# Two plain blocks in place of three at the start of channel mixers 2 to 4, with the Newton steps on GpSimd

## The chip, the core and the metric

The kernel runs on one core of one Trainium2 chip. The metric is the device time of one execution in microseconds (us); lower is better. The core has a matrix engine (TensorE, PE in the profile, with its weight loads as PEld), three vector-like engines (VectorE = DVE, ScalarE = ACT, GpSimd = POOL), an engine that issues transfers (SyncE = SP), and 16 DMA engines between the device memory and the on-chip memory (SBUF). Matmuls write to PSUM, which has 8 banks.

## The reference

A decoder trunk of two layers over 512 positions and 1024 features. Each layer has a channel mixer, a token mixer (latent attention in layer 0, sparse attention in layer 1) and a second channel mixer:

```python
h = h + 0.5 * swiglu(rmsnorm(h, g_a), ...)
h = h + mixer(rmsnorm(h, g_m), ...)
h = h + 0.5 * swiglu(rmsnorm(h, g_b), ...)
def rmsnorm(x, g): return x * rsqrt(mean(x * x, -1) + 1e-6) * g
def swiglu(x, w_gate, w_up, w_down):      # 1024 -> 2816 -> 1024
    return (silu(x @ w_gate) * (x @ w_up)) @ w_down
```

So there are four channel mixers, called mixer 1 to 4 here (`idx` 0 to 3 in the code). The whole is in float32.

## The kernel before

*Layout.* The residual `h` lies as 8 chunks of 128 features by 512 positions. A channel mixer (`ffn`) has 22 blocks `f` of 128 hidden features; each block has a gate and an up product, each of a 1024 x 128 weight slab with all positions.

*Precision.* Every operand is split into a high part (ScalarE's copy to a shorter float format) and a low part (VectorE subtracts the high part), in `split` and `slab_ahead`. A product is then three matmuls: high-high, high-low, low-high.

*Two kinds of blocks.* In a *plain* block (`plain`, `plain1`, L401 to L403) gate and up are computed directly: 2 slabs x 8 chunks x 2 halves of 256 positions x 3 matmuls. In the other blocks (`wsums`, `product`, L386 to L388) gate and up together are seven products of quarter size, in the manner of Strassen and Winograd, each of 4 chunk pairs x 3 matmuls of 256 positions. For these `combine(p)` forms sums of the activations of chunk pair p (`y`, `u`, `four`; L267 to L273 and a split), once per mixer, and `wsums` forms sums of each block's weights (L372 to L376) and splits them. Products 1, 6 and 5 go through one bank (`px`) and 7 and 4 through another (`pq`), with copies by ScalarE between (L554 to L561); 2 and 3 end in the gate's bank (`pg`).

*Norm.* The activations go into the products with the gain but without the norm's factor. Its sums of squares are collected chunk by chunk (`sumsq`, ScalarE and GpSimd); the last two chunks of a mixer's input come in `late`, which ends in small matmuls `pc` and `rsqrt_col`. `rsqrt` makes a first guess from the bits and takes three Newton steps on a 128 x 4 tile (L299 to L304, all on VectorE). `norm_bcast` spreads the column with four transposes (`pb`, L323) and ScalarE copies it to `row`. `gate` multiplies the gate's result by `row`, takes Silu, and multiplies again; `act` forms the hidden activations and splits them.

*Start of a mixer.* The first `PLAIN` = 3 blocks are plain, their gates' banks all held until the row is there; behind them stand the gates, and the combines lie in blocks 0, 1 and 2. In mixer 1 the positions' sums of squares come from a second copy of the input. From block 3 on, each third block (`f % NG == 0`) opens eight `unit`s of the down product of the last three blocks, which are shared out over three blocks; the last blocks' down products stand at the mixer's end, where the next mixer's input is prepared chunk by chunk.

*What sets the order.* Each engine works through a fixed queue. The queues are made by a planner when the program is built: it goes through the program's instructions with the written order as priority, and an engine takes the first that its model holds ready. `issue_after` adds a rule on top: the splits of the block after the first block of products are issued behind `evicted`, the last copy out of `px` in the block before (L561, L365). Transfers of weights are issued by SyncE.

Of the kernel before, what the change touches and what calls it, by code (L numbers as in the profile page):

```python
# [48 lines left out]
PLAIN = 3  # L49
# [12 lines left out]
class Kern:  # L62
# [228 lines left out]
    def rsqrt(self, y, v, t, psum, n):  # L291

        nc = self.nc
        nc.vector.tensor_scalar(v, psum, 1.0 / n, EPS, op0=ALU.mult, op1=ALU.add)
        self.newton(y, v, t)

    def newton(self, y, v, t):
        nc = self.nc
        nc.vector.tensor_scalar(y.bitcast(I32), v.bitcast(I32), 1, None, op0=ALU.logical_shift_right)  # L299
        nc.vector.tensor_scalar(y.bitcast(I32), y.bitcast(I32), -1.0, float(0x5F3759DF), op0=ALU.mult, op1=ALU.add)  # L300
        for _ in range(3):
            nc.vector.scalar_tensor_tensor(t, y, -0.5, v, op0=ALU.mult, op1=ALU.mult)
            nc.vector.tensor_tensor(t, t, y, op=ALU.mult)
            nc.vector.scalar_tensor_tensor(y, t, 1.5, y, op0=ALU.add, op1=ALU.mult)  # L304

# [35 lines left out]
    def wsums(self, idx, f):  # L341
# [3 lines left out]
        if f == PLAIN:  # L345
# [10 lines left out]
        def split(src, pool, tag, bufs):  # L356
# [8 lines left out]
            with self.tc.issue_after(self.evicted.ins) if f == PLAIN + 1 else nullcontext():  # L365
# [61 lines left out]
    def ffn(self, idx, gain_next, ap, tp):  # L427
        nc, a = self.nc, self.a
        self.scr, self.fp = (tp, "sq", 1), tp
# [14 lines left out]
        def act(f):  # L444
            t = tu[f]
            if f < PLAIN:
# [51 lines left out]
        gates = [self.bank("T", "pg") for _ in range(PLAIN)]  # L498
        for f, g in enumerate(gates):
# [12 lines left out]
            if f == 0 and idx > 1:  # L512
                col = late()
            if f == 1 and idx == 0:
                squares(2)
                squares(3)
                col = self.rsqrt_col(sums, D)
            if idx or f:
                self.plain(idx, f, 1, u)
            if f == 0 and idx == 1:  # L520

                col = late()
            if f == 1:
                nc.scalar.activation(self.tiny[:, 4:5], col[:, 0:1], AF.Silu, scale=-1.0)
                pb = self.norm_bcast(col)
                row = tp.tile([P, S], F32, tag="row", bufs=1, name="row")
                self.spread = nc.scalar.activation(row, pb, AF.Copy)
# [6 lines left out]
            for p in (((0,), (1,), (2, 3)) if idx else ((0, 1), (2,), (3,)))[f]:  # L534
                self.combine(p)
# [3 lines left out]

        tail = PLAIN + (NF - 2 - PLAIN) // NG * NG  # L540
        for f in range(PLAIN, NF):
            if f % NG == 0 and f <= tail:
# [991 lines left out]
```

## Time and profile before

| | |
|---|---|
| median of three runs | 1863.17 us (1862.06 to 1864.02) |
| profiled execution | 1862.05 us, its span 1860.3 us |
| granted TensorE clock | 0.999 of full |
| TensorE busy | 1845.7 us (99%), 14464 matmuls |
| VectorE busy | 1507.4 us (81%) |
| ScalarE busy | 1064.5 us (57%) |
| GpSimd busy | 296.7 us (16%) |

Mixer 1 runs from the start to some 355 us, mixer 2 from 546 to 881, mixer 3 from 881 to some 1213, mixer 4 from 1513 on. A row of the instructions in order of time gives the start, the duration, the engine, the source line, the operation, the tile written <- the tiles read, and their shapes; in square brackets stands the idle time of the engine before it and what ended it. Matmuls are pipelined, so their durations overlap; what one costs is read from start to start. Line numbers are those of the kernel before.

### The profile page before, as it was taken

How to read it: one execution, taken by the hardware profiler on the slowest of the kernel's cores; microseconds unless marked ns; L12 is line 12 of the kernel's file. 1: busy time of each engine (PE TensorE's matmuls, PEld its weight loads, DVE VectorE, ACT ScalarE, POOL GpSimd, SP SyncE). 2: the span in 40 equal slices, each digit the busy share in tenths (PEclk: the TensorE clock that was granted, in tenths of full speed). 3: DMA queues.
4: the chain of work that ended last, by engine and by line, in shares of the span. 5: the costliest groups of instructions: out<-in, count | busy, mean ns of one | idle time of the engine just before them, and what ended most of it. 6: DMA issues, size and time to landing. Idle time of an engine off the chain costs nothing.

```text
span 1860.3 us, 37031 instructions
## 1 busy us (share of the span) xinstructions
PE 1845.7 (99%) x14464; PEld 1763.4 (95%) x14464; DVE 1507.4 (81%) x2810; ACT 1064.5 (57%) x1997; POOL 296.7 (16%) x370
## 2 busy tenths in 40 slices
PE   9999999999999999999999999999999999999998
PEld 9999999888889999999999999988888889999997
DVE  8988886688779988886898888666878888888885
ACT  7555553567666555554655545446776865555554
POOL 0000000258830000001000000022666620000000
PEclk9999999999999999999999999999999999999999
DMA  6433331434433433322443332162433133433321
GB/s 238 132 108 103 103 92 48 117 105 103 114 123 112 119 103 109 110 73 72 138 118 110 109 106 81 45 183 82 108 108 103 40 118 116 121 104 107 103 78 69
DMA packets 84351, 196.64 MB, mean 106 GB/s; under 512 B 10944, under 2 KB 38464, under 8 KB 84176
## 3 DMA queue, kind: packets, MB, share of 16 engines
q1 hardware_dynamic: 81664, 191.34, 34.9%
q10 hardware_dynamic: 2512, 2.93, 0.5%
q8 instruction: 114, 1.87, 0.4%
q14 instruction: 61, 0.50, 0.1%
HBM read 178.44 MB, written 2.16 MB: 97 GB/s over the span
## 4 chain that ended last, share of the span: by engine, by line
PE 93%; DVE 3%; ACT 1%; issue 1%; POOL 1%; DMA 0%; ACTq 0%; POOLq 0%; DVEq 0%
PE pd L462 8%; PE pd L464 8%; PE pd L463 8%; PE px L386 6%; PE px L388 6%; PE px L387 5%; PE pg L386 4%; PE pg L388 4%; PE pg L387 4%; PE pq L386 4%; PE pq L388 4%; PE pq L387 4%; PE o L1337 2%; PE pt L1310 2%; PE po L197 2%; PE po L199 2%
## 5 line engine op out<-in xcount | busy, mean ns | idle before, releaser
L462 PE MATMUL pd<-ah,wd 128*128 128x256 f32 x1152 | 318.3, 276 | 0.0
L464 PE MATMUL pd<-ah,wd 128*128 128x256 f32 x1152 | 318.3, 276 | 0.0
L463 PE MATMUL pd<-al,wd 128*128 128x256 f32 x1152 | 318.3, 276 | 0.0
L289 POOL TENSOR_TENSOR s<-s,sq 128x512 f32<-128x512 f32 x38 | 54.7, 1441 | 1050.3 <-ACT sq L285 1050.3
L462 PEld LDWEIGHTS pd<-ah,wd 128*128 128x128 f32 x1152 | 216.3, 188 | 0.0
L464 PEld LDWEIGHTS pd<-ah,wd 128*128 128x128 f32 x1152 | 216.3, 188 | 0.0
L463 PEld LDWEIGHTS pd<-al,wd 128*128 128x128 f32 x1152 | 216.3, 188 | 0.0
L206 DVE TENSOR_TENSOR w<-wr,w 128x1024 fp32r<-128x1024 f32 x72 | 88.2, 1225 | 120.7 <-ACT w L205 120.4
L386 PE MATMUL px<-four,wh 128*128 128x256 f32 x608 | 168.4, 277 | 0.4 <-ACT wh L205 0.2
L388 PE MATMUL px<-four,wl 128*128 128x256 f32 x608 | 168.2, 277 | 0.2 <-DVE wl L206 0.2
L386 PE MATMUL pq<-four,wh 128*128 128x256 f32 x608 | 168.1, 276 | 0.2 <-ACT uq L556 0.2
L387 PE MATMUL px<-four,wh 128*128 128x256 f32 x608 | 168.0, 276 | 0.0
L388 PE MATMUL pq<-four,wl 128*128 128x256 f32 x608 | 167.9, 276 | 0.0
L387 PE MATMUL pq<-four,wh 128*128 128x256 f32 x608 | 167.9, 276 | 0.0
L468 DVE SCALAR_TENSOR_TENSOR h<-pd,h 128x512 f32<-128x512 f32 x216 | 148.3, 686 | 15.4 <-PE pd L464 15.2
L205 ACT ACTIVATE wd<-wdr 128x384 fp32r<-128x384 f32 x192 | 99.2, 519 | 103.8 <-issue 64.6
L176 ACT ACTIVATE w<-wr 128x1024 fp32r<-128x1024 f32 (+3 forms) x89 | 80.8, 908 | 87.5 <-PE pd L464 20.6
L206 DVE TENSOR_TENSOR wd<-wdr,wd 128x384 fp32r<-128x384 f32 x192 | 105.8, 553 | 20.1 <-ACT wd L205 20.0
L178 DVE TENSOR_TENSOR w<-wr,w 128x1024 fp32r<-128x1024 f32 (+3 forms) x75 | 78.3, 1044 | 50.0 <-ACT w L176 49.8
L728 ACT ACTIVATE p<-p,small 128x512 f32<-128x512 f32 (+2 forms) x192 | 106.9, 558 | 19.0 <-DVE small L727 15.3
L386 PEld LDWEIGHTS px<-four,wh 128*128 128x128 f32 x608 | 114.1, 188 | 1.0 <-ACT wh L205 0.4
L388 PEld LDWEIGHTS px<-four,wl 128*128 128x128 f32 x608 | 114.2, 188 | 0.6 <-DVE wl L206 0.6
(379 smaller groups left out, 6264.9 us busy)
## 6 DMA issues: line engine op xcount, KB each, us to landing
wr<-in_w_gu SPq DMA_DIRECT2D x93, 512.0 KB, 3.5
ru<-in_w_gu SPq DMA_DIRECT2D x76, 512.0 KB, 4.3
wdr<-in_w_down SPq DMA_DIRECT2D x192, 192.0 KB, 2.5
wr<-in_w_down SPq DMA_DIRECT2D x24, 256.0 KB, 2.6
wr<-in_mla_w_o SPq DMA_DIRECT2D x8, 512.0 KB, 3.4
th<-btab_d SPq DMA_DIRECT2D x16, 256.0 KB, 3.7
wr<-in_nsa_w_q SPq DMA_DIRECT2D x8, 512.0 KB, 3.8
wr<-in_nsa_w_o SPq DMA_DIRECT2D x8, 512.0 KB, 3.7
```

Source lines behind the costliest of these rows:

```text
L176: self.copied = nc.scalar.activation(wh[:, m], raw[:, m], AF.Copy)
L178: nc.vector.tensor_tensor(wl[:, m], raw[:, m], f32v(wh[:, m]), op=ALU.subtract)
L205: nc.scalar.activation(hi, src, AF.Copy)
L206: (nc.gpsimd if pool else nc.vector).tensor_tensor(lo, src, f32v(hi), op=ALU.subtract)
L386: mm(out, wh[:, p], xh, start=first and p == 0, stop=False, skip_group_check=True)
L387: mm(out, wh[:, p], xl, start=False, stop=False, skip_group_check=True)
L388: mm(out, wl[:, p], xh, start=False, stop=last and p == KP - 1, skip_group_check=True)
L462: nc.tensor.matmul(o, wh, xh, start=k == b0 and x == 0, stop=False, skip_group_check=True)
L463: nc.tensor.matmul(o, wh, xl, start=False, stop=False, skip_group_check=True)
L464: last = nc.tensor.matmul(o, wl, xh, start=False, stop=k == b1 - 1, skip_group_check=True)
L468: nc.vector.scalar_tensor_tensor(self.h[c], p, 0.5, self.h[c], op0=ALU.mult, op1=ALU.add)
L728: nc.scalar.activation(p_sb[:, :n], p_sb[:, :n], AF.Exp, bias=nm, scale=-1.0, accum_out=sm)
```

## The change

Mixer 1 keeps three plain blocks; mixers 2 to 4 (`idx` > 0) have two, so their block 2 is one of seven products. For these mixers the order of the start is written anew: the row (`spread`) is made inside block 1, between its gate and its up slab; each half block is followed by one pair's combine; gate and act of block 0 stand ahead of block 1's up slab. The down units still begin at block 3, and block 2 has none. What hung on `PLAIN` (the buffer of the first weight sums, the wait on `evicted`) now hangs on `self.plains`. In all four mixers the Newton steps go to GpSimd, four instructions per step in place of three, and everywhere the first guess takes one instruction in place of two.

```diff
+        nc.vector.tensor_scalar(y.bitcast(I32), v.bitcast(I32), -0.5, float(0x5F3759DF), op0=ALU.mult, op1=ALU.add)
+        (self.newton_pool if self.to_ffn else self.newton)(y, v, t)
...
     def newton(self, y, v, t):
         nc = self.nc
-        nc.vector.tensor_scalar(y.bitcast(I32), v.bitcast(I32), 1, None, op0=ALU.logical_shift_right)
-        nc.vector.tensor_scalar(y.bitcast(I32), y.bitcast(I32), -1.0, float(0x5F3759DF), op0=ALU.mult, op1=ALU.add)
...
+    def newton_pool(self, y, v, t):
+        e = self.nc.gpsimd
+        for _ in range(3):
+            e.tensor_tensor(t, y, y, op=ALU.mult)
+            e.tensor_tensor(t, t, v, op=ALU.mult)
+            e.tensor_scalar(t, t, -0.5, 1.5, op0=ALU.mult, op1=ALU.add)
+            e.tensor_tensor(y, y, t, op=ALU.mult)
...
-        if f == PLAIN:
+        if f == self.plains:
...
-            with self.tc.issue_after(self.evicted.ins) if f == PLAIN + 1 else nullcontext():
+            with self.tc.issue_after(self.evicted.ins) if f == self.plains + 1 else nullcontext():
...
+        self.plains = 2 if idx else 3
...
+        def spread():
+            nonlocal row
+            nc.scalar.activation(self.tiny[:, 4:5], col[:, 0:1], AF.Silu, scale=-1.0)
+            pb = self.norm_bcast(col)
+            row = tp.tile([P, S], F32, tag="row", bufs=1, name="row")
+            self.spread = nc.scalar.activation(row, pb, AF.Copy)
...
-            if f == 0 and idx > 1:
-                col = late()
...
+            if idx:
+                if f == 0 and idx > 1:
+                    col = late()
+                if f:
+                    spread()
+                self.combine(2 * f)
+                if f:
+                    gate(0, gates[0])
+                    act(0)
                 self.plain(idx, f, 1, u)
-            if f == 0 and idx == 1:
-
-                col = late()
+                if f == 0 and idx == 1:
+                    col = late()
+                self.combine(2 * f + 1)
+                if f:
+                    gate(1, g)
+                    act(1)
+                continue
...
-            for p in (((0,), (1,), (2, 3)) if idx else ((0, 1), (2,), (3,)))[f]:
+            for p in ((0, 1), (2,), (3,))[f]:
                 self.combine(p)
...
-        tail = PLAIN + (NF - 2 - PLAIN) // NG * NG
-        for f in range(PLAIN, NF):
-            if f % NG == 0 and f <= tail:
+        tail, left = (NF - 2) // NG * NG, 1
+        for f in range(self.plains, NF):
+            if f % NG == 0 and NG <= f <= tail:
```

More of the change, by code (lines that the diff above doesn't have):

```diff
@@ L48 @@
 KP = KC // 2
-PLAIN = 3
 PAD = 16
@@ L294, in rsqrt @@
         nc.vector.tensor_scalar(v, psum, 1.0 / n, EPS, op0=ALU.mult, op1=ALU.add)
-        self.newton(y, v, t)
+        nc.vector.tensor_scalar(y.bitcast(I32), v.bitcast(I32), -0.5, float(0x5F3759DF), op0=ALU.mult, op1=ALU.add)
+        (self.newton_pool if self.to_ffn else self.newton)(y, v, t)
     def newton(self, y, v, t):
         nc = self.nc
-        nc.vector.tensor_scalar(y.bitcast(I32), v.bitcast(I32), 1, None, op0=ALU.logical_shift_right)
-        nc.vector.tensor_scalar(y.bitcast(I32), y.bitcast(I32), -1.0, float(0x5F3759DF), op0=ALU.mult, op1=ALU.add)
         for _ in range(3):
@@ L445, in act @@
             t = tu[f]
-            if f < PLAIN:
+            if f < self.plains:
                 t = tu_tile()
@@ L495, in late @@
             return self.norm_col(D, self.s2)
-        gates = [self.bank("T", "pg") for _ in range(PLAIN)]
+        def spread():
[4 more added lines that the diff above has]
+            self.spread = nc.scalar.activation(row, pb, AF.Copy)
+        gates = [self.bank("T", "pg") for _ in range(self.plains)]
         for f, g in enumerate(gates):
@@ L511, in ffn @@
                 self.plain(idx, f, 0, g)
-            if f == 0 and idx > 1:
-                col = late()
[L514 to L518, printed above, removed]
-                self.plain(idx, f, 1, u)
-            if f == 0 and idx == 1:
-                col = late()
+            if idx:
[7 more added lines that the diff above has]
+                    act(0)
+                self.plain(idx, f, 1, u)
+                if f == 0 and idx == 1:
[5 more added lines that the diff above has]
+                continue
+            if f:
+                if f == 1:
+                    squares(2)
+                    squares(3)
+                    col = self.rsqrt_col(sums, D)
+                self.plain(idx, f, 1, u)
             if f == 1:
[L524 to L527, printed above, removed]
+                spread()
                 for e in range(2):
```

## The prediction

> **What bounds the kernel now.** I read the page's busy shares first, then TensorE's own waits, then the windows of the places that the change touches, then the instructions in order of time there.
>
> ```profile
> span 1860.3 us, 37031 instructions
> PE 1845.7 (99%) x14464; PEld 1763.4 (95%) x14464; DVE 1507.4 (81%) x2810; ACT 1064.5 (57%) x1997; POOL 296.7 (16%) x370
> PE pb L323 <- DVE small L304: 1.0, 2, 0.6
> PE pg L386 <- ACT pg L561: 0.3, 1, 0.3
> PE px L388 <- DVE wl L206: 0.2, 1, 0.2
> 1000.00:1100.00 100.00, 100.00 (x885) 100.00 (x884) 85.29 (x133) 52.21 (x86) 0.00 (x0) 1.00 0.37 107
> 881.20:915.70 34.50, 34.33 (x303) 34.13 (x302) 32.24 (x57) 23.67 (x36) 2.60 (x2) 1.00 0.52 166
> ```
>
> The two last rows are stretches: length, then busy time (count) of PE, PEld, DVE, ACT, POOL, then the granted clock. TensorE never pauses: inside a channel mixer it sends 885 matmuls in 100 us, 0.113 us each at full clock, and its waits (engine, line, what it waited for: sum, times, longest) are tenths of a microsecond. So only fewer matmuls, or a new wait of TensorE, move the end. The last row is the start of mixer 3, its three plain blocks: there VectorE is busy 32.24 of 34.5 us. That is where a new wait can come from.
>
> **The change, part by part.**
>
> *Matmuls removed.* A plain block has 2 slabs x 8 chunks x 2 halves x 3 = 96 matmuls of 256 columns, a block of seven products has 7 x 4 x 3 = 84. One block changes kind in each of mixers 2 to 4: 36 matmuls fewer.
>
> ```profile
> 881.17 0.28 PE L401 MATMUL pg<-x,w 128*128 128x256 f32 x1
> 885.93 0.28 PE L401 MATMUL pg<-x,w 128*128 128x256 f32 x1
> 904.70 0.37 PE L401 MATMUL pg<-x,w 128*128 128x256 f32 x1
> 915.69 0.28 PE L386 MATMUL px<-x,w 128*128 128x256 f32 x1
> ```
>
> From the first of these rows to the second are 42 matmuls in 4.76 us, 0.1133 us each (the 0.28 us overlap). 36 x 0.1133 = 4.08 us, 1.36 per mixer. The third plain block runs from 904.70 to 915.69; without it the first block of products starts at about 904.7 and the second, 84 x 0.1133 = 9.5 us later, at 914.2.
>
> *VectorE's work moved earlier.* Its rows in that start, each with start and duration:
>
> ```profile
> 886.25 0.68 DVE L271 TENSOR_TENSOR u<-y 128x512 f32<-128x512 f32 x1
> 886.96 0.43 DVE L272 TENSOR_TENSOR u<-y,u 128x256 f32<-128x256 f32 x1
> 887.31 0.69 DVE L372 TENSOR_TENSOR s<-ru 128x512 f32<-128x512 f32 x1
> 890.05 1.22 DVE L206 TENSOR_TENSOR four<-u,four 128x1024 fp32r<-128x1024 f32 x1
> 891.25 1.22 DVE L178 TENSOR_TENSOR w<-wr,w 128x1024 fp32r<-128x1024 f32 x1
> 905.68 1.23 DVE L178 TENSOR_TENSOR w<-wr,w 128x1024 fp32r<-128x1024 f32 x1 [0.92 <-ACT w L176]
> ```
>
> Instructions overlap by some 0.08 us, so one of 1024 columns costs 1.14, of 512 0.60, of 256 0.34. Needed before the second block of products can run through: four pair sums of 0.60 + 0.34 + 0.34 + 1.14 = 9.7; two plain slabs, 2.3; two blocks' weight sums of 4 x 0.60 + 3 x 1.14 + 0.60 = 6.4 each, the last 0.60 of them later, 12.2; three gates of 4 x 0.60 and 0.68 of product adds, 7.9. Sum 32.1, from 886.25 to 918.3. The last of it feeds product 6 of that block. In written order (1, 7, 6) this is due two products after 914.2, at 916.9; if TensorE's queue has 2 and 4 ahead of 6, at 914.2 + 4 x 1.36 = 919.6. So VectorE is 1.4 us late or 1.3 early, and a bubble such as the 0.92 us of the last row is not in that. TensorE's order is fixed when the program is built and bends to what the planner holds ready: in mixer 1 the copy that ends product 7 (first row below) comes ahead of the one that ends product 1.
>
> *The wait on `evicted`, moved one block ahead.* The splits of the block after the first one of products are issued behind the eviction of that first block (L365). Before, three down units (54 matmuls, 6.1 us) lie between that eviction and the next block; block 2 has no units, so after the change only two products do, 2.7 us.
>
> ```profile
> 42.24 0.38 ACT L556 ACTIVATE uq<-pq 128x256 f32<-128x256 f32 x1 [1.49 <-PE pq L388]
> 44.97 0.37 ACT L554 ACTIVATE pg<-px 128x256 f32<-128x256 f32 x1 [0.28 <-PE px L388]
> 923.15 0.37 ACT L561 ACTIVATE pg<-px 128x256 f32<-128x256 f32 x1 [0.30 <-PE px L388]
> 924.51 1.23 DVE L206 TENSOR_TENSOR w<-wr,w 128x1024 fp32r<-128x1024 f32 x1
> 931.92 1.22 DVE L206 TENSOR_TENSOR wl<-wr,wh 128x1024 fp32r<-128x1024 f32 x1
> ```
> PE pq L386 <- ACT uq L556: 0.2, 1, 0.2
> PE px L386 <- ACT wh L205: 0.2, 1, 0.2
> 32.24 0.62 PE L323 MATMUL pb<-ident,small 128*128 128x128 f32 x4 [0.46 <-issue]
> ```
>
> From the eviction at 923.15 to the end of product 1's lower half (924.51 + 1.23) are 2.6 us: just in time for a block that starts 2.5 us after it. To the end of the last sum's lower half (931.92 + 1.22) are 10.0, of which 1.2 are two adds of down units that will not be there: 8.8 after the eviction, against 5.2 in written order, or 8.0 with 2 and 4 ahead. The lower end is the bare chain on an empty VectorE: copy 0.28, split 0.95 + 1.14, two sums 1.2, split 0.95 + 1.14 = 5.7. So this wait costs between nothing and 3.6 us per mixer. It is the same lateness as VectorE's above, not a second one. I take 0.6: mixer 1 begins as full and its waits (last three rows) are 0.2, 0.2 and 0.46. Three mixers: +1.8.
>
> *Newton by GpSimd.* In the mixers the three Newton steps of `rsqrt` leave VectorE: behind the one on `pc`, 11 small instructions become 1 there and 12 on GpSimd.
>
> ```profile
> 25.05 0.17 DVE L299 TENSOR_SCALAR small<-small 128x4 int32<-128x4 int32 x1
> 888.85 0.15 DVE L294 TENSOR_SCALAR small<-pc 128x4 f32<-128x4 f32 x1
> 897.91 0.17 DVE L304 SCALAR_TENSOR_TENSOR small<-small 128x4 f32<-128x4 f32 x1
> L1146 POOL TENSOR_TENSOR small<-small,gcmp 128x16 f32<-128x16 f32 x4 | 0.9, 226 | 0.1
> 1503.34 1.46 POOL L289 TENSOR_TENSOR s<-s,sq 128x512 f32<-128x512 f32 x1 [0.86 <-ACT sq L285]
> 1503.85 1.50 DVE L209 SCALAR_TENSOR_TENSOR x<-h,ngains,x 128x512 fp32r<-128x512 f32 x1 [0.21 <-ACT x L208]
> 1502.89 0.74 DVE L209 SCALAR_TENSOR_TENSOR x<-h,ngains,x 128x512 fp32r<-128x512 f32 x1
> ```
>
> Before, the chain takes 9.2 us in mixer 3, as each step stands between two large instructions of VectorE, and 10 x 0.08 = 0.8 us of its time. GpSimd's nearest row is 0.226 us: 12 make 2.7 us on a free engine. But the last three rows show that the two engines exclude each other: the same instruction takes 0.74 alone and 1.50 when it starts inside a GpSimd add, just until that ends (1503.34 + 1.46). If each of 12 steps waits out one VectorE instruction (mean 0.7, the mix above) and then holds VectorE up for 0.22, the chain takes 11 us and VectorE loses 2.6 - 0.8 = 1.8 us per mixer. Mixer 1's steps move too: from 25.05 its chain ran up to `pb` at 32.24 (row above), which waited 0.46; ended 3 us after it begins or 11, `pb` gains 0.46 or loses 4. I take nothing there, between the two.
>
> The Trainium skill, page "SBUF — State Buffer", section "Who interferes with whom", states this as a rule: an instruction of VectorE with two SBUF inputs and one of GpSimd that reads SBUF block each other for a whole instruction; the trace agrees (1.50 against 0.74). By that rule alone the sum below would be 1.8 us per mixer higher, +3.1 in all, if VectorE has no slack at all.
>
> *The row half a block earlier.* `spread` now stands behind the gate slab of block 1, its transposes `pb` in TensorE's queue ahead of the up slab's 48 matmuls.
>
> ```profile
> 556.86 0.79 PE pc L311 x8
> 560.29 0.16 DVE L294 TENSOR_SCALAR small<-pc 128x4 f32<-128x4 f32 x1
> 562.93 0.28 PE L403 MATMUL pg<-x,w 128*128 128x256 f32 x1
> 568.80 0.62 PE L323 MATMUL pb<-ident,small 128*128 128x128 f32 x4
> ```
>
> In mixer 3 that place is 881.17 + 0.8 for `pc` + 3 slabs x 48 x 0.1133 = 898.3, 9.4 us after the first small instruction: enough for 0.3 + 2.7, short by 2.0 for 0.3 + 11. I treat mixer 4 like it. In mixer 2 the sums stand behind block 0's up slab, VectorE takes them up at 560.29 and the place is 563.05: 2.8 us later, when 3.0 to 11.3 are needed, so `pb` is 0.2 to 8.5 us late. Where the planner knows the chain's length, it puts `pb` later among the up slab's matmuls and nothing waits. I take +0.3 in mixer 2, near the lower end, and nothing in the others: a planner that orders by readiness is what mixer 1 showed.
>
> *Elsewhere.* One small instruction less in each `rsqrt` of the token mixers too.
>
> ```profile
> 368.70 0.17 DVE L299 TENSOR_SCALAR small<-small 128x4 int32<-128x4 int32 x1
> 370.00 1.26 DVE L300 TENSOR_SCALAR small<-small 128x4 int32<-128x4 int32 x1
> 373.70 0.62 PE L323 MATMUL pb<-ident,small 128*128 128x128 f32 x4 [0.59 <-DVE small L304]
> ```
>
> Here TensorE waits 0.59 us for the chain; without the step that took 1.26 it waits 0 to 0.59 less. I take 0.3. The small tile reads (L538) follow two gates, not three; two weight loads of 512 KB from SyncE change their line and place, not their number, and the DMA engines are half idle there (0.52 in the window's row). The combines' new places behind each half block change the planner's order on VectorE, not the work; I cost them at nothing as long as all four fit, which the 32.1 us count in.
>
> **The sum.** -4.08 + 1.8 + 0.3 - 0.3 = -2.3 us. The profiled execution took 1862.05 us (span 1860.3), 1.1 below the median of the three runs, 1863.17. So 1859.8 for such an execution, 1860.9 for the median. 0.2% is 3.7 us, about what a measurement of this kernel tells from no change.
>
> **The rivals.** *Everything fits (1858.5).* No new wait, and 0.6 us come back in the token mixer: -4.7. For it: TensorE has waits of tenths only in all four starts, its order bends, mixer 1 lives with the same density. Against it: 32.24 of 34.5 us, and less time for it. This is 0.25%, just over the bound.
>
> *The row comes late (1867.2).* GpSimd's chain takes 11 us and TensorE stands before `pb`: the queue is fixed, so all 48 matmuls behind it wait. In mixer 2 that is up to 8.5 us, but VectorE's queue holds the gates, which wait for the row; when it comes to them it stops, and GpSimd runs its last steps freely. I take the middle, 4.4 us, and 2.0 each in mixers 3 and 4. VectorE catches up meanwhile, so the 1.8 fall away: -4.08 - 0.3 + 8.4 = +4.0. It decides from 4.4 us of such waits. For it: the exclusion in the rows, and the 2.7 us in mixer 2. Against: the planner may place `pb` by a chain of the right length, and VectorE's instructions that read PSUM may not exclude GpSimd.
>
> *The sums stay in written order (up to 1869.6).* Each second block waits 3.6 us for product 6, the upper end above; without the 1.8: -4.4 + 10.8 = +6.4, less where down units fill in. Against: mixer 1's order bent.
>
> **How the numbers follow.** The forecast, part of the gain kept, no change that can be told: 0.51, its own range 1859.5 to 1862.7. Everything fits, faster: 0.27. Late row 0.15 and written order 0.07; I put two thirds of these over the bound, 1866.9, giving slower 0.15, same 0.58, and faster 0.27. The range that leaves out 2 in 10 is 1858.3 to 1866.8: the full gain less its tail, and the lower half of the two slow cases.
>
> **What would show it.** TensorE's count falls by 36 to 14428, L386 to L388 rise by 28 x 3 and L401 to L403 fall by 32 x 3. Right: `px` of block 2 starts 23.5 us (904.7 - 881.2) after the first `pg` of each mixer, and TensorE's waits on the weight sums (`wl`, `wh`) stay under 1 us each. Wrong: a wait of `pb` of over 1 us (late row), or of `px` of 3 us behind L206 (written order). GpSimd's small steps show in their starts whether they alternate with VectorE: 0.25 us apart, or 0.9.

## The result, and the profile after

The changed kernel takes 1885.65 us (median of 4 runs, 1884.36 to 1886.4) where the kernel before took 1863.6 beside it: a ratio of 1.0117, 95% interval 1.0102 to 1.0132. It is 22 us slower; the forecast was 2.3 faster. The page of the profiled execution begins with its span and busy shares:

```profile
span 1884.6 us, 37015 instructions
PE 1852.8 (98%) x14428; PEld 1766.7 (94%) x14428; DVE 1518.2 (81%) x2790; ACT 1073.1 (57%) x2012; POOL 319.4 (17%) x418
```

Rows of a run carry the line numbers of that run's kernel. From the waits of the changed kernel (engine, tile, line, what it waited for: sum, times, longest), four of the largest of TensorE's that were not there before, and one of ScalarE's:

```profile
PE pb L329 <- POOL small L310: 6.9, 2, 5.4
PE pu L407 <- ACT w L175: 2.4, 1, 2.4
PE pq L392 <- ACT wh L204: 1.9, 1, 1.9
PE pu L409 <- DVE w L177: 1.6, 2, 0.9
ACT gains L507 <- POOL small L310: 16.7, 4, 6.0
```

The 36 matmuls are gone (14464 to 14428), and yet TensorE is busy 7 us longer. Part of that is a slower clock: the granted clock stood at half for 6.8 us in mixer 2 and for 3.4 us in mixer 3, and a matmul that takes longer counts as busy longer; the rest is not accounted for. At the starts of the mixers, where the longest wait was 0.5 us before, there are now single waits of up to 5.4 us. ScalarE has a new one: its small Silu (L507) stands 16.7 us in four times for the column that GpSimd makes.

Where the time came from is read from the first `pg` of each mixer and TensorE's last row. Each column runs to the next start, so mixer 1's holds the latent attention, mixer 3's the sparse one:

| kernel | mixer 1 | mixer 2 | mixer 3 | mixer 4 |
|---|---|---|---|---|
| before, us | 540.27 | 335.41 | 632.01 | 340.01 |
| after, against before | +6.1 | +8.7 | +6.1 | +3.7 |

Mixer 2 in order of time, GpSimd's steps with VectorE beside them, then ScalarE and TensorE:

```profile
566.65 0.16 DVE L294 TENSOR_SCALAR small<-small 128x4 int32<-128x4 int32 x1
566.89 4.65 POOL L307 TENSOR_TENSOR small<-small 128x4 f32<-128x4 f32 x1 [5.59 <-DVE small L294]
567.06 1.22 DVE L205 TENSOR_TENSOR wl<-ru,wh 128x1024 fp32r<-128x1024 f32 x1
...
570.80 0.68 DVE L205 TENSOR_TENSOR wl<-s,wh 128x512 fp32r<-128x512 f32 x1
571.62 0.20 POOL L308 TENSOR_TENSOR small<-small 128x4 f32<-128x4 f32 x1
571.91 0.19 POOL L309 TENSOR_SCALAR small<-small 128x4 f32<-128x4 f32 x1
...
574.42 0.20 POOL L310 TENSOR_TENSOR small<-small 128x4 f32<-128x4 f32 x1
574.65 0.20 ACT L507 ACTIVATE gains<-small 128x1 f32<-128x1 f32 x1 [5.52 <-POOL small L310]
574.67 1.12 PE L329 MATMUL pb<-ident,small 128*128 128x128 f32 x4 [5.39 <-POOL small L310]
575.83 1.23 DVE L205 TENSOR_TENSOR four<-u,four 128x1024 fp32r<-128x1024 f32 x1 [4.35 <-ACT four L204]
```

and a stretch of 2 us behind it (columns as in the prediction's stretches, the granted clock third from the end):

```profile
576.00:578.00 2.00, 2.00 (x12) 2.00 (x11) 2.00 (x2) 1.98 (x4) 0.00 (x0) 0.50 0.00 0
```

A step that takes 0.20 us on a free engine took 4.65: it began at 566.89 and ended at 571.54, just when VectorE's run of instructions with two SBUF inputs ended (570.80 + 0.68). The other eleven then follow 0.28 us apart. VectorE ended its run only because it had nothing left. Its next instruction needs ScalarE's copy `four`, which stands in ScalarE's queue behind the small Silu, which waits for the column, which waits for VectorE to stop. So VectorE lost 4.35 us, TensorE 5.39, and from 576 to 578 TensorE ran at half the granted clock (0.50 in the stretch): 10 matmuls start in these 2 us, 0.21 us apart, in place of 18 at 0.113. (The 12 of the row count those that reach in from before as well.)

In mixer 3 `pb` does not wait, but the loop is there. The first 23.5 us of the mixer, before and after, and instructions of the latter:

```profile
881.17:904.67 23.50, 23.33 (x206) 23.13 (x205) 22.40 (x42) 17.71 (x26) 2.60 (x2) 1.00 0.57 182
```
```profile
895.92:919.42 23.50, 20.36 (x172) 19.92 (x171) 17.40 (x26) 16.86 (x25) 9.12 (x14) 0.97 0.41 138
```
```profile
904.74 4.26 POOL L307 TENSOR_TENSOR small<-small 128x4 f32<-128x4 f32 x1 [4.45 <-DVE small L294]
914.22 1.23 DVE L205 TENSOR_TENSOR four<-u,four 128x1024 fp32r<-128x1024 f32 x1 [5.28 <-ACT four L204]
916.13 0.39 PE L407 MATMUL pu<-x,w 128*128 128x256 f32 x1 [2.38 <-ACT w L175]
917.39 0.39 PE L409 MATMUL pu<-x,w 128*128 128x256 f32 x1 [0.76 <-DVE w L177]
```

VectorE got 26 instructions done there in place of 42. Ten of the 16 are the small ones that left it; the other six are larger. Its busy time fell by 5.0 us, where the shorter start leaves it little to lose. TensorE stands before a plain slab's split.

### The profile page after: what moved, and what is told of

It reads as the page before. It is cut to its first block, busy times and chain, and to the rows that moved or that the text cites. A ratio compares the mean times of both kernels' runs of the same rounds, so it can differ in the third digit from the quotient of the medians.

```text
span 1884.6 us, 37015 instructions
## 1 busy us (share of the span) xinstructions
PE 1852.8 (98%) x14428; PEld 1766.7 (94%) x14428; DVE 1518.2 (81%) x2790; ACT 1073.1 (57%) x2012; POOL 319.4 (17%) x418
## 4 chain that ended last, share of the span: by engine, by line
PE 87%; DVE 5%; ACT 2%; POOL 1%; issue 1%; DMA 0%; POOLq 0%; DVEq 0%; ACTq 0%
PE pd L471 8%; PE pd L469 8%; PE pd L470 8%; PE px L392 6%; PE px L394 5%; PE px L393 5%; PE pg L392 4%; PE pg L394 4%; PE pg L393 4%; PE pq L392 4%; PE pq L394 4%; PE pq L393 4%; PE o L1360 2%; PE pt L1333 2%; PE po L196 2%; PE po L198 2%
## 5 line engine op out<-in xcount | busy, mean ns | idle before, releaser
L392 PE MATMUL px<-four,wh 128*128 128x256 f32 x632 | 176.7, 280 | 3.0 <-ACT wh L204 1.7
L392 PE MATMUL pq<-four,wh 128*128 128x256 f32 x632 | 174.9, 277 | 1.9 <-ACT wh L204 1.9
L394 PE MATMUL px<-four,wl 128*128 128x256 f32 x632 | 175.1, 277 | 0.3 <-DVE wl L205 0.3
L393 PE MATMUL px<-four,wh 128*128 128x256 f32 x632 | 174.8, 277 | 0.0
L394 PE MATMUL pq<-four,wl 128*128 128x256 f32 x632 | 174.7, 276 | 0.0
L393 PE MATMUL pq<-four,wh 128*128 128x256 f32 x632 | 174.7, 276 | 0.0
L392 PEld LDWEIGHTS px<-four,wh 128*128 128x128 f32 x632 | 118.7, 188 | 5.6 <-ACT wh L204 2.6
L175 ACT ACTIVATE w<-wr 128x1024 fp32r<-128x1024 f32 (+3 forms) x83 | 74.4, 897 | 81.8 <-PE pd L471 17.9
L392 PEld LDWEIGHTS pq<-four,wh 128*128 128x128 f32 x632 | 118.7, 188 | 2.3 <-ACT wh L204 2.3
L394 PEld LDWEIGHTS px<-four,wl 128*128 128x128 f32 x632 | 118.7, 188 | 0.5 <-DVE wl L205 0.5
L393 PEld LDWEIGHTS px<-four,wh 128*128 128x128 f32 x632 | 118.7, 188 | 0.0
```

The source lines that it names most:

```text
L175: self.copied = nc.scalar.activation(wh[:, m], raw[:, m], AF.Copy)
L392: mm(out, wh[:, p], xh, start=first and p == 0, stop=False, skip_group_check=True)
L393: mm(out, wh[:, p], xl, start=False, stop=False, skip_group_check=True)
L394: mm(out, wl[:, p], xh, start=False, stop=last and p == KP - 1, skip_group_check=True)
```

## The experiments

All kernels are timed against the kernel before on the same chip (medians 1863.2 to 1864.2). "The layout" is all of the change but `rsqrt`: two plain blocks in mixers 2 to 4, early row, new places of the combines.

### The Newton steps

*Newton back on VectorE, and GpSimd's Newton alone on the kernel before.*

```diff
# the changed kernel, Newton on VectorE
-        (self.newton_pool if self.to_ffn else self.newton)(y, v, t)
+        self.newton(y, v, t)
# the kernel before, rsqrt and newton_pool of the change, nothing else
+        (self.newton_pool if self.to_ffn else self.newton)(y, v, t)
```

> The kernel after, with the Newton steps of the channel mixers back on VectorE (the one-instruction first guess stays). Theory A (GpSimd's chain is kept out by VectorE's run of instructions with two SBUF inputs; TensorE at pb and ScalarE at the small Silu stand behind it): no GpSimd step is left to starve, each step fits between two large instructions, the waits of 5.4 us in mixer 2, 2.4 in mixer 3 and 1.5 to 1.9 in mixer 1 go: 1860 to 1866 us. Theory B (two plain blocks leave VectorE too little time, whoever does Newton): 1880 us or more. Theory C (the row's early place, a third of the loss each): 1870 to 1878 us.

> The kernel before with one part of the change alone: the Newton steps of the channel mixers on GpSimd; three plain blocks, row behind block 1's up slab, combines as before. Theory A: mixer 1 loses the same 6 us as in the kernel after, since it is the same program there; in mixers 2 to 4 the row is wanted 5.4 us later than in the kernel after, so 0 to 4 us each: 1868 to 1880 us. Theory B: no change, 1861 to 1865 us. Theory C: mixer 1's 6 us alone, 1869 us.

Measured: 1872.46 us (ratio 1.0047, 1.0031 to 1.0063) and 1877.74 (1.0075, 1.0059 to 1.0091). The first is above the 1866 that was the most expected of theory A: something of 8.5 us is left without GpSimd. GpSimd's steps cost 13.2 us in the new layout. In the old one guess and steps together cost 13.8, the steps alone 12.2 (against the guess alone, the next run). So they are most of the result, and not bound to two plain blocks. By mixer, each figure from two profiled executions, which makes 14.6 and 13.0 in all:

| what the steps cost, us | mixer 1 | mixer 2 | mixer 3 | mixer 4 |
|---|---|---|---|---|
| new layout (changed kernel less Newton on VectorE) | 3.5 | 5.4 | 5.0 | 0.7 |
| old layout (steps and guess less guess alone) | 4.3 | 4.0 | 3.6 | 1.1 |

A step that is passed over for 4 us is not needed for the loss. In mixer 1 of the changed kernel no step takes over 1.06 us, and in mixer 3 of the old layout the first one takes 0.57. Where the steps stand also changes the planner's order of the other instructions; what that order costs by itself no run separates.

*The first guess alone, on the kernel before.*

```diff
+        nc.vector.tensor_scalar(y.bitcast(I32), v.bitcast(I32), -0.5, float(0x5F3759DF), op0=ALU.mult, op1=ALU.add)
-        nc.vector.tensor_scalar(y.bitcast(I32), v.bitcast(I32), 1, None, op0=ALU.logical_shift_right)
-        nc.vector.tensor_scalar(y.bitcast(I32), y.bitcast(I32), -1.0, float(0x5F3759DF), op0=ALU.mult, op1=ALU.add)
```

> The kernel before with the one-instruction first guess alone, everywhere. In e1 mixer 1 was 2.6 us longer than before though only this instruction differs there. Theory A': a 0.08 us instruction less is worth at most 1 us: 1862 to 1864 us, and mixer 1's 2.6 us in e1 came from something else. Theory D: the planner's order shifts, mixer 1 is 2 to 3 us longer again, other mixers by 0 to 2: 1864 to 1869 us.

Measured: 1865.54 (1.0007, 0.9997 to 1.0016), as a whole not to be told from nothing. The trace says more. Mixers 2 to 4 are within 0.1 us of those before, and mixer 1 is 2.6 us longer, as it is with Newton on VectorE in the new layout (also 2.6). In both, the missing instruction gives mixer 1 another order, and block 3 waits in the same two places. With Newton on VectorE:

```profile
42.69 0.39 PE L394 MATMUL px<-x,w 128*128 128x256 f32 x1 [1.51 <-DVE w L205]
44.97 0.38 PE L392 MATMUL pq<-four,wh 128*128 128x256 f32 x1 [0.73 <-ACT wh L204]
```

With the guess alone these are 1.49 and 0.72 us; the kernel before has only 0.25 there. So some 2 us of the 2.6 are the new order, which is what theory D expected.

*The small Silu of ScalarE reads a constant*, so that it no longer waits for the column.

```diff
-            nc.scalar.activation(self.tiny[:, 4:5], col[:, 0:1], AF.Silu, scale=-1.0)
+            nc.scalar.activation(self.tiny[:, 4:5], f32v(self.ones)[:, 0:1], AF.Silu, scale=-1.0)
```

> The kernel after, but the one-column Silu that stands ahead of the row reads a constant in place of Newton's column, so that ScalarE waits for nothing there; the row itself is unchanged. Under theory A there are two ways by which the late column costs time: TensorE at pb, and ScalarE's queue, which stands at the Silu and holds back splits behind it. If ScalarE's queue is the way in mixers 3 and 4 (where pb waits for nothing long but the up slab waits for ScalarE's split), 6 to 10 us come back: 1875 to 1880 us. If only pb matters: 1884 to 1887 us, no change. Theory B: no change.

Measured: 1889.05 (1.0127, 1.0108 to 1.0145). No gain, and above every range that was expected. So the time does not hang on the loop through the Silu alone. ScalarE now feeds VectorE, VectorE does not stop, and GpSimd is kept out longer; in mixer 2 the row's wait grows from 5.39 us:

```profile
576.33 1.10 POOL L310 TENSOR_TENSOR small<-small 128x4 f32<-128x4 f32 x1
577.51 1.06 POOL L307 TENSOR_TENSOR small<-small 128x4 f32<-128x4 f32 x1
580.58 1.11 PE L329 MATMUL pb<-ident,small 128*128 128x128 f32 x4 [7.15 <-POOL small L310]
```

*VectorE held while GpSimd works*: one small instruction of VectorE reads the finished column.

```diff
             e.tensor_tensor(y, y, t, op=ALU.mult)
+        self.nc.vector.tensor_scalar(t[:, 0:1], y[:, 0:1], 1.0, 1.0, op0=ALU.mult, op1=ALU.mult)
```

> The changed kernel with one small VectorE instruction added behind each mixer's Newton steps: it reads the finished column, so VectorE stands there until GpSimd's last step is done. In mixer 2 it lies three instructions (two of 256 columns, one of 1024, some 1.8 us) behind the instruction that makes the first guess. Theory A (GpSimd's step is locked out as long as VectorE runs instructions with two SBUF inputs back to back, and only for so long): GpSimd's first step ends when VectorE stops, 1.6 to 2.0 us after it began in place of 4.65 (mixer 2) and 4.26 (mixer 3); the 11 steps behind it are 0.25 to 0.3 us apart; the chain ends 4.6 to 5.3 us after the first guess, and pb waits 2 to 3 us in mixer 2 in place of 5.39. VectorE stands 3 us in each mixer for it, so the time gains only part of that: 1880 (1875 to 1886) against 1885.7. Rival B (GpSimd's first step is slow by itself, as its engine has to wake up or its instruction to be fetched): the first step still takes over 4 us although VectorE stands, pb waits over 7 us, and the time is over 1888.

```profile
567.24 1.44 POOL L307 TENSOR_TENSOR small<-small 128x4 f32<-128x4 f32 x1 [5.59 <-DVE small L294]
567.41 1.22 DVE L205 TENSOR_TENSOR wl<-ru,wh 128x1024 fp32r<-128x1024 f32 x1
571.79 0.15 DVE L311 TENSOR_SCALAR small<-small 128x1 f32<-128x1 f32 x1 [3.17 <-POOL small L310]
571.82 0.65 PE L330 MATMUL pb<-ident,small 128*128 128x128 f32 x4 [2.18 <-POOL small L310]
574.27 0.39 PE L410 MATMUL pu<-x,w 128*128 128x256 f32 x1 [1.57 <-DVE w L177]
915.17 0.39 PE L410 MATMUL pu<-x,w 128*128 128x256 f32 x1 [2.95 <-DVE w L177]
1544.81 0.39 PE L410 MATMUL pg<-x,w 128*128 128x256 f32 x1 [1.97 <-DVE w L177]
```

That VectorE's run holds up GpSimd's step is shown: the first step now ends after 1.44 us, with the instruction behind which VectorE stops (567.41 + 1.22 = 568.63), and `pb` waits 2.18. Rival B, a step that is slow by itself, falls. As a whole the time is not won: 1884.99 (1.0116, 1.01 to 1.0133). VectorE stands 3.17 us in place of GpSimd, and TensorE waits for its slabs instead (1.57, 2.95, 1.97). By mixer it is not even: mixer 2, where the other instructions of VectorE, ScalarE and TensorE are in the same order in both kernels, is 2.5 us shorter than in the changed kernel and mixer 3 is 1.3 shorter; mixer 4, where GpSimd had its turns before, is 2.2 longer. That fits with a hold that pays where a step would be passed over and costs where it would not, but it is one profile of each.

### The row

*The row behind block 1's up slab, in the changed kernel and in the layout alone.*

```diff
-                if f:
-                    spread()
                 self.combine(2 * f)
-                if f:
-                    gate(0, gates[0])
-                    act(0)
                 self.plain(idx, f, 1, u)
...
+                if f:
+                    spread()
+                    gate(0, gates[0])
+                    act(0)
                 self.combine(2 * f + 1)
```

> The kernel after with the row (and gate and act of block 0) behind block 1's up slab, as before the change; two plain blocks and GpSimd's Newton stay. Theory C (the early place is the loss): the waits at pb in mixers 2 to 4 go, 1866 to 1872 us. Theory A: pb gets 5.4 us more, enough for mixer 2's 5.4 us, but mixer 1's 6 us stay and ScalarE still stands at the Silu: 1872 to 1880 us. Theory B: 1880 us or more, as the gates only come later.

> e5 with the row, gate and act of block 0 behind block 1's up slab, as before the change. In e1 TensorE waited 2.5 us at pb in mixer 2, where the sums stand behind block 0's up slab. Theory C (the early row is what is left): that wait goes, 3 to 5 us under e5. Theory A' (VectorE short of time): the gates come later and the waits move to the products, within 2 us of e5.

Measured: 1883.02 (1.0104, 1.0088 to 1.012) and 1868.32 (1.0022, 1.0012 to 1.0031): 2 to 3 us gained on the kernel with the early row, though in both pairs the intervals overlap. The first is above what was expected of theory A: TensorE no longer waits at `pb` in mixer 2, but there for a plain slab (1.09 us) and a copy (2.67). With Newton on VectorE, `pb` in mixer 2 waits 1.21 us in place of 2.57.

### The layout

*The layout alone*, `rsqrt` as before.

```diff
-        nc.vector.tensor_scalar(y.bitcast(I32), v.bitcast(I32), -0.5, float(0x5F3759DF), op0=ALU.mult, op1=ALU.add)
-        (self.newton_pool if self.to_ffn else self.newton)(y, v, t)
+        self.newton(y, v, t)      # with its two instructions of the first guess
```

> The kernel after with the whole of rsqrt as before (two-instruction first guess, Newton on VectorE): two plain blocks, early row, the new places of the combines. Mixer 1 and the token mixers are then the program of before. Theory A' (GpSimd's chain cost 13 us; what was left in e1, 8.5 us over before, is the start of mixers 2 to 4, too short for VectorE): mixer 1 loses nothing, mixers 2 to 4 as in e1 (+3.3, +1.1, +2.9): 1869 to 1872 us. Theory D (what was left is the planner's order, shifted by the missing instruction): near the forecast without GpSimd, 1859 to 1863 us.

Measured: 1870.36 (1.0029, 1.0018 to 1.004), 6.3 us over the kernel before, with 36 matmuls (4.08 us) fewer. So the layout loses some 10 us. In mixer 2 it is the row. In mixer 3, ScalarE's queue, VectorE and TensorE:

```profile
572.08 0.79 PE L322 MATMUL pb<-ident,small 128*128 128x128 f32 x4 [2.57 <-DVE small L303]
912.84 0.68 DVE L448 SCALAR_TENSOR_TENSOR tu<-pu,tg 128x512 f32<-128x512 f32 x1
913.55 0.63 ACT L204 ACTIVATE ah<-tu 128x512 fp32r<-128x512 f32 x1 [0.57 <-DVE tu L448]
914.09 0.37 ACT L570 ACTIVATE pg<-px 128x256 f32<-128x256 f32 x1
914.51 0.38 PE L385 MATMUL pg<-x,w 128*128 128x256 f32 x1 [1.16 <-ACT pg L570]
915.86 0.39 PE L385 MATMUL px<-four,wh 128*128 128x256 f32 x1 [0.61 <-ACT wh L204]
```

The 26.5 us behind mixer 3's two plain blocks, and the same stretch of that mixer in the kernel before:

```profile
910.58:937.08 26.50, 24.70 (x197) 23.26 (x197) 24.58 (x38) 14.85 (x24) 0.00 (x0) 1.00 0.32 95
```
```profile
904.67:931.17 26.50, 26.39 (x232) 26.19 (x231) 21.78 (x32) 14.95 (x25) 0.00 (x0) 1.00 0.31 95
```

The copy out of `px` for which TensorE waits begins at 914.09; the last matmul of its product was issued at 911.72. It stands in ScalarE's queue behind a copy `ah` that waits for VectorE's `tu`. And VectorE is busy 24.58 of 26.5 us there, before 21.78.

*Three plain blocks again, with the rest of the layout; and the same with the row of mixer 2 late.*

```diff
-        self.plains = 2 if idx else 3
+        self.plains = 3
-            if idx:
+            if idx and f < 2:
...
# and the second kernel: spread, gate 0 and act 0 of mixer 2 behind the up slab
-                if f:
+                if f and idx > 1:
```

> e5 with three plain blocks in all mixers: early row and the combines' new places stay, block 2 is plain and has no combine. Theory A' (too little time before the first block of products): 10.9 us more for VectorE, the waits on split weights go, 1862 to 1865 us, the 4.1 us of matmuls given back. Theory C or D (early row, or any new order): 1866 us or more, the waits stay although there is time.

> The kernel with three plain blocks in all mixers, the combines' new places and the early row (1865.5), with the row of mixer 2 late again, as its sums of squares come later there; mixers 3 and 4 keep it early. Nothing of the layout with two blocks is left. If the wait of 2.4 us at mixer 2's row and the half clock behind it were all that kept that kernel from the one before: mixer 2 as before (335.4), 1862.0 (1860.5 to 1864), level with it or up to 0.1 % under. If the combines' places in blocks 0 and 1 cost by themselves: 1864.5 to 1866.

Measured: 1865.5 (1.0007, 0.9998 to 1.0016) and 1862.26 (0.9994, 0.9985 to 1.0003). With the third block the waits in mixers 3 and 4 are gone but for 0.4 us (those mixers are 0.9 and 0.4 us shorter than before), and mixer 2 carries 2.41 us at `pb`, +3.9 in all; with its row late it is +0.2. The second kernel has the lowest median of all, but cannot be told from the kernel before.

*Which queue it is.* Seven kernels, five here and two below, try to tell VectorE's load from ScalarE's order. The five: the rule on `evicted` back at block 4; block 1's up slab written behind block 2's products; gates and activations written behind them, and the same with the row ahead; and block 2's first copy ahead of its last weight splits:

```diff
# the rule back (on the late row)
-            with self.tc.issue_after(self.evicted.ins) if f == self.plains + 1 else nullcontext():
+            with self.tc.issue_after(self.evicted.ins) if f == 4 else nullcontext():
# up slab as filler: row, gates and up slab behind block 2's products (the next kernel, copies first: the same without the two lines of the up slab)
+            if f == 2 and idx:
+                spread(); gate(0, gates[0]); act(0)
+                for k in self.order:
+                    self.plain1(up, k, tu[1])
             gate(f, g)
+            if f == 2 and idx:
+                act(2); gate(1, gates[1]); act(1)
+                continue
...
# copies first, row before: spread() ahead of wsums of block 2, gate and act 0 behind its second copy
# first copy first (on the late row)
+            first = nc.scalar.activation(g[:, :HS], x, AF.Copy)
+            if f == 2 and idx:
+                with self.tc.issue_after(first.ins):
+                    self.rest()      # splits of w[6], w[3] and w[5]
```

> The kernel with two plain blocks, Newton on VectorE and the late row (1868.3), with one edit: the rule that puts the splits of a block behind the last copy out of px applies to block 4 again, as before, and not to block 3. The prediction put this rule's move at 0.6 us per mixer, +1.8, between nothing and 3.6 each. If it costs that: 1866.5 (1864.5 to 1867.2), with shorter waits in blocks 3 and 4. If the waits are those of ScalarE's copies in block 2 alone: no difference, 1867.3 to 1869.3. If the rule helped, in that it keeps VectorE's order: over 1869.3.

> Two plain blocks, first guess and Newton on VectorE as before the change, and in mixers 2 to 4 block 1's up slab written behind the products of block 2 (row, gates 0 and 2, then gate 1 behind it), so that its 48 matmuls lie in TensorE's queue between the products. Theory C (with the Newton steps away, what the layout loses is that nothing lies between block 2's products: the copies out of px and pq by ScalarE, 0.37 us each, and the row's wait show on TensorE, 2 to 3 us per mixer): the waits of px and pg behind ScalarE's copies in block 2 (0.86 to 1.16 us in the kernels with the layout alone) and pb's wait (1.2 to 2.6 in mixer 2) fall under 0.3 us each, and each of mixers 2 to 4 is 2 to 3 us shorter than in the kernel with the late row (1868.3): 1861.5 (1859 to 1864.5), level with the kernel before or up to 0.25 % under it. Rival D (VectorE lacks the time for sums, slabs and gates, whatever stands between): the same total of waits comes back as waits on weight sums and slabs from VectorE (px, pq or pu behind L205 or L177 for over 1 us in each mixer), 1866 to 1870.

> Two plain blocks with first guess and Newton on VectorE, and in mixers 2 to 4 the row, the gates and the hidden activations of blocks 0 and 1 written behind block 2's seven products, so that ScalarE's copies out of px and pq and the weight sums come ahead of them in every queue. Nothing is left out. Theory E (the copies for which TensorE waits stand in ScalarE's queue behind copies of hidden activations that wait for VectorE; in the kernel with the early row the copy at 914.09 stood behind two such): the waits of px and pg behind ScalarE's copies in block 2 (0.86 to 1.51 us in the kernels with the layout alone) fall under 0.3, and each of mixers 2 to 4 is 1 to 2 us shorter than with the late row (1868.3): 1863.5 (1861 to 1866). Theory D (VectorE is short altogether): a wait of the same size moves on to block 3, whose bank and down units need the gates and activations that now come later: pg or pd of block 3 waits 2 us or more per mixer, 1867 to 1873.

> As the kernel with the copies first, but the row is written ahead of block 2's weight sums (its transposes stand at the end of block 1 in TensorE's queue), and gate and activation of block 0 stand behind block 2's first two copies. Theory E: the copies' waits in block 2 stay under 0.5 us and block 3 has its bank and activations earlier: 1862.5 (1860 to 1865.5). Theory D: as the layout with the late row, 1866.5 to 1870, with the waits on weight sums or on the activations (px or pg behind L205, pd behind L205) in place of those on copies.

> Two plain blocks, late row, Newton on VectorE (1868.3), with one more edit: in block 2 of mixers 2 to 4 ScalarE makes the copy out of px behind product 1 ahead of the last three weight splits of that block, which in the other kernels stand ahead of it and wait for VectorE's sums. Theory E (the order of ScalarE's queue): px's waits behind that copy (0.86, 0.50 and 1.04 us in mixers 2, 3 and 4) go, nothing of their size comes in their place: 1866.0 (1864 to 1867). Theory F (there are two late things in a row, the copy and the weight sums that VectorE makes for product 6; each kernel shows the later one): the waits come back behind the splits of the weight sums (px behind wh L204 or w, wl L205), 0.5 us or more in two of the three mixers: 1867.2 to 1870.

Measured, in this order: 1870.84 (1.0038, 1.0025 to 1.0051), 1872.47 (1.0049, 1.0036 to 1.0063), 1881.49 (1.0091, 1.0077 to 1.0104), 1870.71 (1.0034, 1.0021 to 1.0048), 1871.64 (1.0045, 1.0032 to 1.0057). None is faster than the late row alone (1868.32), and all but the first are above every range that was expected of them. With the rule on `evicted` back at block 4 the kernel is no faster, so its move cost nothing that this shows. With the up slab as filler, the copies no longer hold TensorE, but the weight sums do (`pq` behind `wl`: 1.72, 1.88 and 0.76 us). In the slowest, with the copies first, the waits move on to block 3 (in mixers 2 and 4 each 0.63 us for an activation, 1.19 and 0.63 to 0.76 for weight sums), and the clock stands at half there for 3.4 and 6.8 us. With the first copy forced ahead its wait goes, and waits on weight sums and activations come, 0.36 to 0.64 us.

*Less work for VectorE*, on the layout alone: one, then both multiplications by the row left out in blocks 0 to 3.

```diff
# one
+            if idx == 0 or f > 3:
                 nc.vector.tensor_tensor(t, t, row, op=ALU.mult)
# both
+            if idx and f <= 3:
+                nc.scalar.activation(t, g, AF.Silu, scale=-1e-4)
+                return
```

> The layout alone (two plain blocks, early row, first guess and Newton on VectorE as before; 1870.4), with the second multiplication by the row left out in blocks 0 to 3 of mixers 2 to 4: four VectorE instructions of 512 columns, 0.60 us each, 2.4 us of VectorE's work per mixer, none of TensorE's or ScalarE's. Theory D (VectorE is what is short in the shorter start; in mixer 3 it runs from 902.6 to 917 without a gap, and TensorE's wait for ScalarE's copy at 913.1 is VectorE's lateness, passed on through an `ah` copy that waits for `tu` ahead of it): TensorE's waits in blocks 2 to 4 shrink by 1 to 2.4 us per mixer in mixers 3 and 4 and by about 1 in mixer 2, where the row's wait at the Newton steps stays: 1866.0 (1863.5 to 1867.8). Theory C (the copies' own latency shows, as no down units lie between block 2's products, whatever VectorE does): the waits of px and pg behind ScalarE's copies stay, no more than 0.5 us gained per mixer: 1869 to 1871.

> The layout alone (1870.4), with both multiplications by the row left out in blocks 0 to 3 of mixers 2 to 4 (ScalarE takes Silu straight from the gate's bank): eight VectorE instructions of 512 columns, 0.60 us each, 4.8 us of VectorE's work per mixer, twice as much as with one of the two left out (1868.4). The gates' banks also no longer wait for the row; the row's transposes and their wait in mixer 2 (2.57 us) stay. Theory D (VectorE is short, by 1.9 to 3.3 us per mixer): with more taken away than is lacking, TensorE's waits in blocks 2 to 4 of mixers 3 and 4 fall to those of the kernel before (0.5 us), 2.5 to 3.5 us less per mixer, and by 1 to 1.5 in mixer 2: 1862.5 (1860 to 1865). Theory C (between block 2's products lies too little for the round through ScalarE, whatever VectorE does): the waits of px and pg behind ScalarE stay at 1 us or more in mixers 3 and 4, 1867 to 1869.

Measured: 1868.41 (1.0025, 1.0016 to 1.0035) and 1869.59 (1.003, 1.0019 to 1.0042). With 2.4 us less work for VectorE in each of three mixers 1.9 us came back in all, with 4.8 us less only 0.8, and the intervals of all three overlap. Mixer 3 of the second:

```profile
911.40 0.53 ACT L204 ACTIVATE wd<-wdr 128x384 fp32r<-128x384 f32 x1 [3.50 <-DMA wdr<-in_w_down]
913.15 1.06 ACT L204 ACTIVATE wh<-rg 128x1024 fp32r<-128x1024 f32 x1 [1.23 <-DVE rg L375]
914.12 0.61 ACT L204 ACTIVATE ah<-tu 128x512 fp32r<-128x512 f32 x1
914.63 0.37 ACT L573 ACTIVATE pg<-px 128x256 f32<-128x256 f32 x1
915.05 0.39 PE L385 MATMUL px<-four,wh 128*128 128x256 f32 x1 [2.86 <-ACT pg L573]
```

The same copy stands behind a split that waited 3.50 us for a transfer of down weights, one that waited for VectorE, and `ah`; the matmul that it frees waited 2.86. So the theory that VectorE's load alone is at fault falls, and so does the theory that one place in ScalarE's queue is. What is shown: with two plain blocks something between block 2's products comes late in every order tried: a copy, behind whatever in ScalarE's queue is late at that point, or, where the copy is not late, a weight sum or an activation. With the third plain block none of this is seen. Which of these chains would have to be shortened first is open.

## Why the prediction was wrong, by its steps

*Matmuls removed*: right, 14428.

*Newton by GpSimd*: this step failed, by 13 us. Its bound for the chain held: 2.7 to 11 us were said, and it took 4.8, 7.7, 7.3 and 6.1 in mixers 1 to 4. But the chain has no term of its own in the sum. Mixers 1, 3 and 4 were put at nothing, mixer 2 at 0.3 for a late `pb`, and VectorE's loss of 1.8 us per mixer was named and left out. Measured, the steps cost 13.2 us, 3.5 of them in mixer 1. What was overlooked is what else waits for the column. ScalarE's small Silu does, first in `spread`, with all of ScalarE's queue behind it, and so VectorE, which stood 2.89, 4.35, 5.28 and 2.96 us behind it in mixers 1 to 4. That is the way that the rows of the changed kernel show. It is not the only one: with the Silu out of the loop, or VectorE held, the waits move and the time stays. Shown is that the time goes with the steps' place on GpSimd, and that VectorE's run holds up a step; how much of the 13.2 us is this exclusion and how much the planner's other order is open. The late-row rival had the right sign (1867.2, chance 0.15), and the sign that it named, a wait of `pb` of over 1 us, came in mixers 1 and 2; but it let VectorE catch up while TensorE stands, and VectorE stood too. In mixers 3 and 4 `pb` did not wait at all.

One row that the step rests on was misread. The instruction of 1.50 us does not end just with GpSimd's add (1503.34 + 1.46 = 1504.80) but at 1503.85 + 1.50 = 1505.35, 0.55 us behind it. That it was held up is seen all the same, as the same instruction took 0.74 just before.

*Mixer 1 as a whole* became 6.1 us longer: 3.5 by the steps and 2.6 by the shorter first guess, of which some 2 us are the new order (the guess alone, above). The rest can be spread between executions: of eleven kernels with the guess of before, and so with its mixer 1, nine take 0.7 to 1.5 us longer there in their profiles, and two 2.2 and 3.5. The prediction put the shorter guess at a small gain.

How the steps alternate was half right. In mixer 4, where the steps cost least, they did take turns:

```profile
1542.03 0.57 POOL L307 TENSOR_TENSOR small<-small 128x4 f32<-128x4 f32 x1 [3.70 <-DVE small L294]
1542.46 1.22 DVE L205 TENSOR_TENSOR four<-u,four 128x1024 fp32r<-128x1024 f32 x1
1542.68 1.06 POOL L308 TENSOR_TENSOR small<-small 128x4 f32<-128x4 f32 x1
```

In mixers 2 and 3 one step stayed out through a whole run. The rule that the prediction named from the Trainium skill, page "SBUF — State Buffer", section "Who interferes with whom", that the two block each other for a whole instruction, agrees with the trace as a lower bound (1.06 us behind one instruction of 1.22); a step that gets no turn for a whole run, 4.65 us here, is more than it says.

*The row half a block earlier*: +0.3 was the lower end of 0.2 to 8.5, and wrong for mixer 2: 2.57 us of wait even with the old chain (2.41 with three plain blocks), and half clock behind it, 3.9 us in all. "Nothing" in mixers 3 and 4 was right (-0.9 and -0.4 with three plain blocks).

*VectorE's work and the wait on `evicted`*, +1.8: mis-sized, and in the wrong place. With the late row, mixers 2 to 4 are 2.4, 0.8 and 1.5 us longer than before with 1.36 us of matmuls less each: 3.7 + 2.1 + 2.9 = 8.7 us lost in one profile. The waits of TensorE that the trace shows in the first 60 us of these mixers are 5.7 us, before 0.9; the rest is not accounted for. The forecast looked for them at the weight sums, which are 0.8 of it; 3.2 stand at ScalarE's copies, which it did not follow through their queue, and 1.2 at `pb`. The rule on `evicted` cost nothing that a run shows.

*The token mixers*, -0.3: nothing; `pb` there waits 0.63 us, before 0.59. *The combines' places*, nothing: right (the last kernel with three plain blocks).

Taken one after the other, 13.2 (Newton), 2.1 (first guess, from the two kernels without GpSimd's steps; 1.5 on the kernel before, uncertain) and 6.3 (layout) make 21.6 of the 22.05. They must, as each is the difference to the next kernel. In the other order guess and steps are 13.8 on the kernel before, which leaves 8.3 for the layout, so the parts shift by some 2 us with what else is there.

## What to carry to other kernels

When a small chain moves to another engine, give it a term of its own, and list everything that waits for its result, in every queue, and what stands behind each waiter; a loop through an engine that holds up the new one is only seen that way. One small instruction less can cost more than it saves where it gives the planner another order. A stage that exists to cover others (the third plain block) is worth its own time plus every wait that it hides, so price its removal by walking each in-order queue through the first products behind it. Where a sum of busy times says "just fits", expect the waits to surface at the engine between, here ScalarE's copies, and not where the late engine's own operands are due.

## What the runs showed of the hardware

A GpSimd step of 0.20 us that waits for VectorE's instructions with two SBUF inputs can be passed over through five to seven of them (4.65 and 4.26 us) or get its turn after one (0.57, 1.06); what decides is not shown. Free, the small steps of 0.20 us follow 0.28 us apart.

After TensorE stood for 2.57 us the granted clock fell to half (first row below, the layout alone, mixer 2), and so it did after 1.72 us in the kernel with the up slab as filler. The length of the pause alone does not decide: in mixer 1 of the changed kernel and of the kernel before with GpSimd's steps, TensorE stood 1.92 and 1.93 us at the same place, and the clock stayed whole in the first (next row; the wait is the one of `pq` on `wh` in its waits above) and fell in the second (last two). Within the programs it stayed at half for 3.4 us each time, or for twice or three times that.

```profile
574.00:575.50 1.50, 1.50 (x9) 1.50 (x9) 0.72 (x2) 1.47 (x5) 0.00 (x0) 0.50 0.19 16
46.50:49.50 3.00, 3.00 (x24) 2.89 (x25) 3.00 (x7) 1.43 (x3) 0.00 (x0) 1.00 0.52 142
45.63 0.38 PE L393 MATMUL pq<-four,wh 128*128 128x256 f32 x1 [1.93 <-ACT wh L205]
46.50:49.50 3.00, 3.00 (x14) 3.00 (x15) 3.00 (x7) 1.06 (x1) 0.00 (x0) 0.50 0.51 156
```

The Trainium skill, page "TensorE: Matmul & The Clock Gate", part 1, gives an idle window of about 3.4 us for this; here a shorter pause sufficed.
